# The order of the 32 small block products per pair of heads: head by head, or alternating

## The chip, the cores and the metric

The kernel runs on one core of a Trainium2 chip. The time is the device time of that core in microseconds (us), the median of several executions. Five engines work side by side, each through its own queue in order: TensorE (matmuls; PE in the profile, its weight loads PEld), VectorE (DVE), ScalarE (ACT), GpSimd (POOL) and SyncE (SP, which issues DMA transfers). They wait for each other by semaphores. Matmuls write PSUM; TensorE reads SBUF, and the other engines carry results from PSUM back to SBUF.

## The reference

A decoder trunk of two residual layers over 512 positions and 2048 channels. Layer one is gated differential attention, layer two gated RWKV-7 time mixing with 32 heads of 64 channels. What matters here is the scan of layer two, per head with state S:

```python
def step(S, inp):
    r_t, w_t, k_t, v_t, a_t, b_t = inp
    sa = jnp.einsum('bhvk,bhk->bhv', S, a_t)
    S = S * w_t[:, :, None, :] + sa[..., None] * b_t[:, :, None, :] + v_t[..., None] * k_t[:, :, None, :]
    y = jnp.einsum('bhvk,bhk->bhv', S, r_t)
    return S, y

_, ys = lax.scan(step, jnp.zeros((B, H, N, N), F32), xs)
```

Around it stand the projections `p = h @ w_in` (2048 x 8192 and some low-rank parts), a shift by one position, a normalisation per head, a gate and the projection `o @ w_out`. All of it is in float32.

## The kernel before

**Projections.** A large float32 product is made from three products of rounded parts (high by high, high by low, low by high): `mm3`, line 122. Weights come by DMA, ScalarE casts a group to its high part (`wh`, line 105) and VectorE subtracts it from the original to get the low part (`wl`, line 106). These L122 matmuls of 512 columns fill most of TensorE's time.

**The scan in chunks.** Layer two (`layer1`) takes the 32 heads as 16 pairs, head 0 of a pair on partitions 0 to 63 and head 1 on 64 to 127. The 512 positions are 8 chunks of 64. Within a chunk the recurrence is a triangular system of 64 x 64, and its inverse T is made ahead of the scan. For each pair:

- `gram` (L1304) multiplies keys by queries into the tiles `gp`, one for each head and half of the chunks; ScalarE copies them into G (L1311); sums of squares go the same way (L1210, L1211, copied at L1291). The 32 x 32 diagonal blocks go by DMA to memory (`ltd`).
- `t_solve` (L1350 to L1365) loads the diagonal blocks of all chunks and heads and inverts them on VectorE in 31 steps (L1361, L1363).
- `t_combine` puts the inverted blocks into TT by DMA, transposes the first block of each chunk on VectorE (T1, L1388), and makes the block between the two diagonal ones by two products of 32 x 32 per chunk and head. Phase one (L1394) multiplies a block of G by T1 into one half of the tile px. ScalarE copies the result to X (L1397), once per head. It also copies queries from AR over the part of G of that head that the products have read (L1400, once per head). Phase two (L1404) multiplies X by a block of TT into the other half of px, and ScalarE copies that into TT (L1407).
- `scan_pair` then goes through the chunks: L1475 (G by VS), a copy to rhs (L1478), L1486 (T by rhs), a copy to VS (L1488), L1493 (the next state), which VectorE scales and adds (L1497). `outputs` (L1515, L1519) and `centre` follow.

**Placing on the array.** The products of phase one use a 32 x 32 part of TensorE's array: rows 0 to 31 and columns 32 to 63 for head 0, rows 64 to 95 and columns 96 to 127 for head 1. Phase two uses rows 32 to 63 and columns 0 to 31 for head 0, and rows 96 to 127 and columns 64 to 95 for head 1. px is one PSUM tile of 128 x 512 (tag "pd", one buffer); the heads write different partitions of it.

**What sets the order.** A pair's chain (`chain`, `Chain.step`) is a generator that yields between its steps. Every L122 matmul of the projections that go on meanwhile counts the chain's wait down (`tick`), and when it is used up the next step's instructions are put behind that matmul (`issue_after`). GAP_D, GAP_X and GAP_T (18, 10 and 8 matmuls) are the waits in `t_combine`. All steps have a raised priority (SCAN), the casts of weights a lower raised one (AHEAD), parts of `gram` and `t_solve` a higher one (SOLVE). The queue of each engine is written at compile time by a planner: it goes through the program with its own costs for each instruction and, at each engine, takes of those that are ready the one with the highest priority, then the earliest in the program. It inserts the waits that the data need. Tiles in PSUM are tracked as wholes: the copies to X read one head's part of px, but come after both heads' products.

Two bursts per pair are meant below by "burst": the 32 instructions (each float32 product is two) of L1394 and the 32 of L1404.

Of the kernel before, what the change touches and what calls it, by code (L numbers as in the profile page):

```python
# [1137 lines left out]
NC_ = T // C  # L1138
# [233 lines left out]
def t_combine(g, j, p, lead):  # L1372

    nc, w, TT = g.nc, g.work, g.TT[j % 2]
    for h in range(2):
        for half in range(2):
            o, l0 = half * HALF, half * 16 + h * NC_
            nc.sync.dma_start(
                out=TT[h * C + o : h * C + o + HALF, :, h, o : o + HALF],
                in_=g.td[j % 2].rearrange("q (g l) t -> (q g) l t", g=NG)[:, l0 : l0 + NC_, :])  # L1380
    T1 = w.tile([P, NC_, HALF], F32, name="T1", tag="T1", bufs=1)
    X = w.tile([P, NC_, HALF], F32, name="X", tag="X", bufs=1)
    px = g.ps.tile([P, 512], F32, name="px", tag="pd", bufs=1)
    yield lead
    for h in range(2):
        r_ = slice(h * C, h * C + C)
        with g.tc.issue_after(g.centred) if g.centred else ExitStack():
            nc.vector.transpose(T1[r_], TT[r_, :, h, 0:HALF])  # L1388
    yield GAP_T
    N = NC_ * HALF  # L1390
    blocks = [(h, h * C, slice(h * C, h * C + HALF), slice(h * C + HALF, h * C + C)) for h in range(2)]
    for h, b0, lo, hi in blocks:
        for c in range(NC_):
            nc.tensor.matmul(px[hi, c * HALF : (c + 1) * HALF], p.G[lo, c, 0, h, HALF:C], T1[lo, c, :],  # L1394
                             start=True, stop=True, tile_position=(b0, b0 + HALF))
    for _, _, _, hi in blocks:
        nc.scalar.copy(X[hi], px[hi, :N].rearrange("p (c s) -> p c s", c=NC_))  # L1397
    for h, b0, _, _ in blocks:
        r_ = slice(b0, b0 + C)
        nc.scalar.copy(p.G[r_, :, 0, h, :], p.AR[r_, :, 0, :])  # L1400
    yield GAP_X
    for h, b0, lo, hi in blocks:
        for c in range(NC_):
            nc.tensor.matmul(px[lo, N + c * HALF : N + (c + 1) * HALF], X[hi, c, :], TT[hi, c, h, HALF:C],  # L1404
                             start=True, stop=True, tile_position=(b0 + HALF, b0))
    for h, b0, lo, _ in blocks:
        nc.scalar.copy(TT[lo, :, h, HALF:C], px[lo, N:].rearrange("p (c s) -> p c s", c=NC_))  # L1407
    yield GAP_T
# [46 lines left out]
def chain(g, j, p, delay, gap, gap_s, others=(), lead=GAP_D - GAP_T):  # L1455
    def steps():
        yield from t_combine(g, j, p, lead)
        yield from scan_pair(g, j, p, gap, gap_s, dict(others))

    p.chain = Chain(g, steps(), delay)  # L1460
    return p.chain
# [310 lines left out]
```

## Time and profile before

| | |
|---|---|
| median of 3 runs | 2113.84 us (2110.9 to 2114.43) |
| the profiled execution | 2111.84 us, span 2110.1 us |
| granted TensorE clock | 0.997 |
| busy: PE, DVE, ACT, POOL | 98%, 76%, 55%, 18% of the span |
| L1394, both heads | 512 instructions in 16 pairs, 18.1 us busy |
| L1404, both heads | 512 instructions in 16 pairs, 17.7 us busy |

The span is from the first to the last instruction of the profiled execution. In the groups by line, a row has the line, engine and operation, the tile written and those read, the shape, the count, then busy time in us, mean length of one in ns, and the idle time before them with what ended it. Busy time counts overlapping instructions once. A matmul's record is longer than the time until the next may start, so a group's busy time over its count is less than the mean of one. In a timeline a row has the start and length in us, the engine, the line, and how many consecutive instructions are merged; in brackets how long the engine was idle before, and what ended that.

### The profile page before, as it was taken

The numbers are of one execution on the slowest core, as the hardware profiler recorded it, in microseconds if no ns is written. First come the engines' busy times: TensorE is split into PE (matmuls) and PEld (weight loads), VectorE is DVE, ScalarE is ACT, GpSimd is POOL, SyncE is SP. The second block draws the span as 40 slices with busy tenths as digits, with TensorE's granted clock in tenths as the row PEclk, the third lists the DMA queues.
The fourth block names the chain that finished last, engine by engine and source line by source line (L and its number), as shares of the span: only waits on it lengthen the run. The fifth ranks groups of instructions, "written<-read, shape, count | busy, mean of one in ns | idle before, by whom it ended". The sixth has DMA issues, their size and how long they took to land.

```text
span 2110.1 us, 34038 instructions
## 1 busy us (share of the span) xinstructions
PE 2076.8 (98%) x11852; PEld 1690.5 (80%) x11852; DVE 1602.6 (76%) x4129; ACT 1153.6 (55%) x2278; POOL 370.4 (18%) x727
## 2 busy tenths in 40 slices
PE   9999999999999999999999999999999999999999
PEld 7888888888887788878777778888877787877887
DVE  6988888889887876576777778877777887767645
ACT  5765656566565544355465555565555556555322
POOL 1021111201112000101122221222222122221001
PEclk9999999999999999999999999999999999999999
DMA  8487877878778946623232332323333232345655
GB/s 268 153 173 190 181 170 187 166 188 177 173 183 176 307 149 179 150 88 96 90 87 89 90 90 84 94 83 92 99 95 86 85 94 86 97 138 180 190 159 121
DMA packets 159484, 294.60 MB, mean 140 GB/s; under 512 B 64352, under 2 KB 81760, under 8 KB 159312
## 3 DMA queue, kind: packets, MB, share of 16 engines
q1 hardware_dynamic: 110848, 184.91, 28.1%
q0 software_dynamic: 23808, 83.54, 21.5%
q10 hardware_dynamic: 24656, 23.97, 3.5%
q8 instruction: 93, 1.52, 0.3%
q14 instruction: 79, 0.65, 0.1%
HBM read 268.71 MB, written 23.66 MB: 139 GB/s over the span
## 4 chain that ended last, share of the span: by engine, by line
PE 74%; DVE 17%; issue 3%; ACT 3%; DMA 2%; ACTq 0%; DVEq 0%; SPq 0%
PE pp L122 33%; PE pp L568 22%; PE pt L122 4%; DVE wl L106 4%; DVE tmpl L1361 3%; DVE Tm L1363 2%; DVE VS L1497 2%; PE gp L1304 1%; ACT wh L105 1%; PE sc L122 1%; PE o L122 1%; PE sm L1475 1%; PE lora L122 1%; PE z L122 1%; PE sm L1486 1%
## 5 line engine op out<-in xcount | busy, mean ns | idle before, releaser
L106 DVE TENSOR_TENSOR wl<-wraw,wh 128x1024 fp32r<-128x1024 f32 (+2 forms) x291 | 357.7, 1229 | 211.0 <-ACT wh L105 202.2
L105 ACT CAST wh<-wraw 128x1024 fp32r<-128x1024 f32 (+2 forms) x291 | 303.6, 1043 | 266.1 <-PE pp L122 135.2
L122 PE MATMUL pp<-hL,wh 128*128 128x512 f32 x1024 | 414.7, 405 | 0.0
L122 PE MATMUL pp<-hH,wh 128*128 128x512 f32 x1024 | 413.8, 404 | 0.0
L122 PE MATMUL pp<-hH,wl 128*128 128x512 f32 x1024 | 413.6, 404 | 0.0
L122 PEld LDWEIGHTS pp<-hH,wh 128*128 128x128 f32 x1024 | 193.6, 189 | 34.3
L122 PEld LDWEIGHTS pp<-hL,wh 128*128 128x128 f32 x1024 | 193.5, 189 | 33.3
L122 PEld LDWEIGHTS pp<-hH,wl 128*128 128x128 f32 x1024 | 193.6, 189 | 32.4
L568 PE MATMUL pp<-wh,hH 128*128 128x512 f32 x448 | 176.8, 395 | 0.0
L568 PE MATMUL pp<-wh,hL 128*128 128x512 f32 x448 | 175.8, 392 | 0.0
L122 PE MATMUL pp<-wh,hH 128*128 128x512 f32 x372 | 145.6, 392 | 1.8 <-ACT hH L1092 1.8
L122 PE MATMUL pp<-wh,hL 128*128 128x512 f32 x372 | 146.4, 394 | 0.2
L122 PE MATMUL pp<-wl,hH 128*128 128x512 f32 x372 | 145.9, 392 | 0.5 <-DVE wl L106 0.5
L1481 POOL COPY SA<-VS 64x64 f32<-64x64 f32 x224 | 69.9, 312 | 425.0 <-DVE VS L1497 386.0
L1361 DVE SCALAR_TENSOR_TENSOR tmpl<-LT,Tm 128x60 f32<-128x60 f32 (+24 forms) x496 | 133.6, 269 | 11.4
L568 PE MATMUL pp<-wl,hH 128*128 128x512 f32 x448 | 140.4, 392 | 0.0
L1363 DVE TENSOR_TENSOR Tm<-Tm,tmpl 128x60 f32<-128x60 f32 (+24 forms) x496 | 104.4, 211 | 11.3
L1478 ACT COPY rhs<-sm 64x64 f32<-64x64 f32 x256 | 52.8, 206 | 89.3 <-PE sm L1475 85.9
L568 PEld LDWEIGHTS pp<-wl,hH 128*128 128x128 f32 x448 | 84.4, 188 | 17.3
L568 PEld LDWEIGHTS pp<-wh,hH 128*128 128x128 f32 x448 | 84.2, 188 | 17.3 <-issue 0.3
L568 PEld LDWEIGHTS pp<-wh,hL 128*128 128x128 f32 x448 | 84.2, 188 | 16.3
L1488 ACT COPY VS<-sm 64x64 f32<-64x64 f32 x256 | 52.7, 206 | 71.9 <-PE sm L1486 67.3
(397 smaller groups left out, 4417.6 us busy)
## 6 DMA issues: line engine op xcount, KB each, us to landing
wraw<-in_rw_w_in_dram SPq DMA_DIRECT2D x128, 512.0 KB
wraw<-in_da_w_in_dram SPq DMA_DIRECT2D x75, 512.0 KB
wraw<-in_da_w_in_dram POOLq DMA_DIRECT2D x28, 512.0 KB, 6.6
wraw<-in_da_w_out_dram SPq DMA_DIRECT2D x26, 512.0 KB
wraw<-in_rw_w_out_dram SPq DMA_DIRECT2D x26, 512.0 KB
Ta<-in_da_w_in_dram POOLq DMA_DIRECT2D x21, 512.0 KB, 5.5
Tb<-in_da_w_in_dram POOLq DMA_DIRECT2D x21, 512.0 KB, 5.5
Tc<-in_da_w_in_dram POOLq DMA_DIRECT2D x21, 512.0 KB, 5.5
```

The source lines that it names most:

```text
L105: a = nc.scalar.copy(hi[:, ks], raw[:, ks])
L106: d = nc.vector.tensor_sub(lo[:, ks], raw[:, ks], hi[:, ks].bitcast(F32))
L122: m = nc.tensor.matmul(out, a, b, start=s, stop=e, skip_group_check=skip)
L568: m = nc.tensor.matmul(out[t][:], x, wt[lo][:, k, :], start=first, stop=end and lo == 1 and k == KG - 1, skip_group_check=True)
L1304: m = nc.tensor.matmul(gp[h][:, i * P : (i + 1) * P], BK[r_, c0 + i, :, :], p.AR[r_, c0 + i, :, :], start=True, stop=True)
L1361: nc.vector.scalar_tensor_tensor(tt, LT[:, i : i + 1, i + 1 :].to_broadcast([P, s, n]), n2[:, i : i + 1], Tm[:, 0:s, i : i + 1].to_broadca ...
L1363: nc.vector.tensor_add(Tm[:, 0:s, i + 1 :], Tm[:, 0:s, i + 1 :], tt)
L1475: nc.tensor.matmul(sm[:, 0:P], both(p.G[:, c, 0]), both(VS[:, c]), start=True, stop=True)
L1478: nc.scalar.copy(rhs[r_, :], sm[r_, h * C : h * C + C])
L1481: nc.gpsimd.tensor_copy(p.SA[r_, c - 1, :], VS[r_, c, h, :])
L1488: g.copied = nc.scalar.copy(VS[r_, c, h, :], sm[r_, P : P + C])
L1497: g.state = nc.vector.scalar_tensor_tensor(VS[r_, c + 1, h, :], s_, p.gam[r_, c : c + 1], Sg[r_, :], ALU.mult, ALU.add)
```

## The change

In both phases the two loops change places: the outer one is now over the 8 chunks, the inner one over the 2 heads. Each product keeps its operands, its place on the array and its place in px. The copies around them keep their order in the program.

```diff
-    for h, b0, lo, hi in blocks:
-        for c in range(NC_):
+    for c in range(NC_):
+        for h, b0, lo, hi in blocks:
             nc.tensor.matmul(px[hi, c * HALF : (c + 1) * HALF], p.G[lo, c, 0, h, HALF:C], T1[lo, c, :],
                              start=True, stop=True, tile_position=(b0, b0 + HALF))
...
     yield GAP_X
-    for h, b0, lo, hi in blocks:
-        for c in range(NC_):
+    for c in range(NC_):
+        for h, b0, lo, hi in blocks:
             nc.tensor.matmul(px[lo, N + c * HALF : N + (c + 1) * HALF], X[hi, c, :], TT[hi, c, h, HALF:C],
                              start=True, stop=True, tile_position=(b0 + HALF, b0))
```

## The prediction

> **What bounds the kernel now.** First the head of the profile's page, for the engines' shares; then the groups of instructions by line, for the two lines that the change touches; then the stages by windows; then, around one of these places, the timelines of TensorE and ScalarE, which decide.
>
> ```profile
> span 2110.1 us, 34038 instructions
> PE 2076.8 (98%) x11852; PEld 1690.5 (80%) x11852; DVE 1602.6 (76%) x4129; ACT 1153.6 (55%) x2278; POOL 370.4 (18%) x727
> ```
>
> TensorE is busy 98% of the span, ScalarE 55%: by the averages any matmul time that is saved would be time saved. The two groups:
>
> ```profile
> L1304 PE MATMUL gp<-AR,BK 64*128 64x128 f32 x512 | 33.4, 279 | 0.7 <-DVE AR L1279 0.7
> L1394 PE MATMUL px<-T,G 32*32 32x32 f32 x512 | 18.1, 192 | 2.0 <-DVE y L1418 1.2 <-DVE T L1388 0.8
> L1404 PE MATMUL px<-TT,X 32*32 32x32 f32 x512 | 17.7, 192 | 0.0
> ```
>
> L1394 is phase one and L1404 phase two. Each product is two instructions here, so one head's eight chunks are 16 and a burst of both heads is 32; 512 make 16 bursts of each, one per pair of heads. All the small products together are 35.8 us, 1.7% of the span: that is the most there is to win from.
>
> Eleven of the 16 pairs form a steady state, with bursts from 1250.09 to 1864.22 us. The first and the last of its ten full periods, by windows (length, then PE, PEld, DVE, ACT and POOL busy, clock, DMA):
>
> ```profile
> 1250.09:1311.56 61.47, 60.67 (x422) 49.40 (x421) 46.42 (x130) 35.06 (x78) 15.24 (x35) 1.00 0.30 90
> 1802.79:1864.22 61.43, 60.75 (x422) 49.40 (x421) 45.29 (x128) 34.76 (x77) 15.27 (x35) 1.00 0.38 112
> ```
>
> Some 0.7 to 0.8 us of each period has no matmul, and busy time hides more, since a matmul's record is longer than its slot. Where TensorE waits is seen in its timeline at one of these pairs (start, length, line):
>
> ```profile
> 1557.16 1.09 PE L1394 MATMUL px<-T,G 32*32 32x32 f32 x32
> 1558.42 0.40 PE L1211 MATMUL pt<-sLx,ones 128*2 128x512 f32 x1
> 1558.74 2.06 PE L1304 MATMUL gp<-AR,BK 64*128 64x128 f32 x32
> 1560.73 1.09 PE L1404 MATMUL px<-TT,X 32*32 32x32 f32 x32
> ...
> 1564.85 0.40 PE L122 MATMUL pp<-hH,wh 128*128 128x512 f32 x1
> 1565.08 0.40 PE L122 MATMUL pp<-hL,wh 128*128 128x512 f32 x1
> 1565.41 0.43 PE L1486 MATMUL sm<-rhs,TT 128*128 128x64 f32 x2
> ```
>
> L122 matmuls start 0.23 us apart, yet the first step of the scan that needs T, L1486, starts 0.33 after its predecessor: TensorE waits about 0.10 there. ScalarE's timeline says for what:
>
> ```profile
> 1554.04 0.69 ACT L1132 ACTIVATE mixr<-pp,omu 128x512 f32<-128x512 f32 x1
> 1557.88 0.62 ACT L1400 COPY G<-AR 64x512 f32<-64x512 f32 x1 [3.15 <-PE px L1394]
> 1558.53 0.36 ACT L1397 COPY X<-px 32x256 f32<-32x256 f32 x1
> 1558.91 0.57 ACT L1291 COPY ssl<-pt 2x512 f32<-2x512 f32 x1
> 1559.51 0.36 ACT L1397 COPY X<-px 32x256 f32<-32x256 f32 x1
> 1559.90 0.61 ACT L1400 COPY G<-AR 64x512 f32<-64x512 f32 x1
> 1560.54 0.62 ACT L1101 CAST sHx<-mixr 128x512 fp32r<-128x512 f32 x1
> 1561.18 2.06 ACT L1311 COPY G<-gp 128x512 f32<-128x512 f32 x4
> 1563.09 0.74 ACT L1407 COPY TT<-px 32x256 f32<-32x256 f32 x2
> 1563.86 1.05 ACT L105 CAST wh<-wraw 128x1024 fp32r<-128x1024 f32 x1
> 1564.93 0.42 ACT L1478 COPY rhs<-sm 64x64 f32<-64x64 f32 x2
> ```
>
> From L1400 at 1557.88 to the end of L1478 at 1565.35 ScalarE has no gap: 7.47 us of work in a fixed order, and L1486 follows 0.06 behind it. So over the 8.25 us from the burst to L1486 the limit is **ScalarE's row of copies**, and not TensorE. What starts the row is head 0 alone: L1400 copies into the part of G that head 0's products of phase one read, and it comes 0.72 after the burst's start, while the burst's last matmul ends at 1.09. In the brackets stands how long ScalarE had been idle, and for whom.
>
> **The change, part by part.** Nothing is added or taken away: the same 512 matmul instructions of each line, the same copies, no DMA on any queue. Only the order within each burst changes.
>
> *How long an alternated burst takes.* No row shows it, so it is bounded. Where the two heads' halves stand apart, one head alone takes:
>
> ```profile
> 1188.11 0.69 PE L1394 MATMUL px<-T,G 32*32 32x32 f32 x16
> 1189.92 0.69 PE L1394 MATMUL px<-T,G 32*32 32x32 f32 x16
> ```
>
> Less 0.19 for the last record (L1394's mean), 15 steps take 0.50, 0.033 each. Lower end: both heads run at once, 0.69. Upper end: no overlap at all, 31 x 0.033 + 0.19 = 1.22. Today's 1.09 lies 0.13 under that: at the one change of head in the burst the second head starts while the first still runs, in the same px tile. The nearest row for steady alternation is L1304, which goes head by head within each chunk already: 32 instructions of 128 columns in 2.06 us, 0.058 each, while the same number of columns on the whole array takes 0.11 (L1475, two in 0.22 of the chain of waits, row below). That is two heads at a time. I take **0.70**: a burst is 0.39 us shorter, and 32 bursts would give 12.5.
>
> ```profile
> 1563.87 0.22 PE sm L1475 x2
> ```
>
> A rule of the Trainium skill speaks against this. The Trainium skill, TensorEngine Tiling (Array Packing), Restrictions and Gotchas, says that different row tiles cannot use one PSUM bank at the same time. The two heads here are different row tiles and both write px, whereas L1304 writes a tile per head. By that rule a burst would take 1.22 and the sum would be the second rival's below; the 0.13 of overlap in today's burst, in px too, contradicts it for a few matmuls.
>
> *What it is worth in the eleven steady pairs.* TensorE would come to L1404 0.39 earlier (X is ready then: its second copy ends at 1559.87, and L1404 would be due at 1560.34) and to L1486 0.78 earlier. There it meets ScalarE's row, whose length does not depend on this order. Its start does: head 0's last product is now the third last instruction of the burst, but if the heads run at once it still ends 0.69 to 0.70 after the start, and L1400 comes at 0.72 to 0.73. So L1486 stays at 8.25 and the wait before it grows from 0.10 to 0.88. Worth per pair: 0, bounds -0.05 (copies in another order overlap better) and +0.06 (heads hinder each other a little). I take +0.01: 11 x 0.01 = +0.1.
>
> *In the first three pairs* ScalarE has no full row; L1478 itself waits for TensorE (idle before it, in brackets):
>
> ```profile
> 1033.89 0.42 ACT L1478 COPY rhs<-sm 64x64 f32<-64x64 f32 x2 [1.51 <-PE sm L1475]
> 1085.24 0.42 ACT L1478 COPY rhs<-sm 64x64 f32<-64x64 f32 x2 [1.52 <-PE sm L1475]
> 1142.51 0.42 ACT L1478 COPY rhs<-sm 64x64 f32<-64x64 f32 x2 [1.04 <-PE sm L1475]
> ```
>
> There the saving passes on: 4 bursts x 0.39 = 1.56 in the first two. The third pair has its phase two cut by a scan step, so 0.39 for phase one and between 0 and 0.39 for the rest, say 0.20.
>
> ```profile
> 1141.34 0.71 PE L1404 MATMUL px<-TT,X 32*32 32x32 f32 x20
> 1141.98 0.49 PE L1475 MATMUL sm<-VS,G 128*128 128x128 f32 x2
> 1142.40 0.56 PE L1404 MATMUL px<-TT,X 32*32 32x32 f32 x12
> ```
>
> *In the fourth pair*, quoted above, the planner already ran head 0's 16 alone, since head 1's T1 was not there, and it will again: nothing in phase one. In phase two ScalarE's row stands in the way as in the steady state. Worth 0.
>
> *In the last pair* phase one is cut the same way. In phase two the cast that precedes L1478 waits for TensorE, so 0.39 passes on:
>
> ```profile
> 1928.08 1.05 ACT L105 CAST wh<-wraw 128x1024 fp32r<-128x1024 f32 x1 [0.67 <-PE pp L122]
> ```
>
> **Sum**, on the profiled execution of 2111.84 us (span 2110.1): -1.56 - 0.59 - 0.39 + 0.1 = -2.4, so 2109.4. The median of the runs shown is 2.0 above that execution, so the forecast for it is 2113.84 - 2.4 = **2111.4**, 0.11% less. I call anything within 0.2% (4.2 us) no change, about what a measurement of this kernel can tell.
>
> **Rivals.**
>
> *The steady pairs gain too.* The order on ScalarE is fixed at compile time by a planner that looks at what is ready. Head 0's copies become ready half a burst later in its eyes, which can move other copies. If the cast L105 (1.05 us) fell behind L1478, ScalarE's row would end early enough for TensorE's full 0.88 per pair: 11 x 0.88 = 9.7, with the 2.4 above 2101.7. If only L1101 (0.62) fell behind, 6.8 and 2104.6. For it: in the second pair L1478 has no cast ahead of it. Against it: in the fourth pair the row runs 0.6 us later against its burst (L1407 at 6.52 instead of 5.93) and the planner still put L1101 and L105 ahead of L1478:
>
> ```profile
> 1193.15 0.62 ACT L1101 CAST sHx<-mixr 128x512 fp32r<-128x512 f32 x1
> 1193.67 1.07 ACT L1311 COPY G<-gp 128x512 f32<-128x512 f32 x2
> 1194.63 0.73 ACT L1407 COPY TT<-px 32x256 f32<-32x256 f32 x2
> 1195.38 1.05 ACT L105 CAST wh<-wraw 128x1024 fp32r<-128x1024 f32 x1
> 1196.46 0.42 ACT L1478 COPY rhs<-sm 64x64 f32<-64x64 f32 x2
> ```
>
> *The heads do not overlap: slower.* If alternate matmuls run one after the other, head 0 is done after 29 x 0.033 + 0.19 = 1.15 instead of 0.69. L1400 and the whole row behind it come 0.46 later, and L1486 with them: 11 x 0.46 = 5.1. Seven bursts without that cover (six early, one in the last pair) lose 0.13 each, 0.9. Together +6.0: 2119.8. It decides as soon as a head's step grows so that its 15 steps take 0.4 us longer. For it: the two heads share px, and L1304 does not show that case. Against it: the overlap at the change of head.
>
> *The planner puts something more into the row: slower.* A ScalarE instruction of 0.6 us or more that the planner now finds ready while head 0's copies are not would push L1486 by its length: 0.69 (as L1132 before the burst) x 11 = 7.6, less 2.4: 2119.0. It outweighs the gain from 0.22 us up. For it: the planner sees half a burst more of idle time. Against it: ScalarE sat idle 3.15 us before L1400 and the planner found nothing to put there.
>
> **How the numbers follow.** Forecast (order kept, heads overlap, the steady pairs take the gain back) 0.55; steady pairs gain 0.23; no overlap 0.11; a longer row 0.11. The forecast's own range is 2109.5 to 2114.5: the early gains whole (-3.3 with -0.05 per steady pair) or only 1 us of them (with +0.06), and the runs' own spread around their median. The range for 8 in 10 takes in the faster rival and the nearer slower one: 2101.0 to 2119.0. Faster by over 0.2%: 0.22 of the first rival and 0.07 of the forecast, where the spread adds to the gain, 0.29. Slower: 0.20 of the two slower rivals. Within: 0.51.
>
> **What would show it.** Right: L1394 and L1404 bursts of 32 at 0.70 instead of 1.09; L1400 still 0.72 behind the burst; the wait before L1486 near 0.9 in the steady pairs; periods still 61.4 long. Wrong: bursts at 1.1 or more with L1400 at 1.2 (no overlap), or L1478 ahead of L105 or L1101 with periods near 60.5. The forecast fails most easily if the planner's order on ScalarE moves, since the whole steady state hangs on what stands between L1400 and L1478.

## The result, and the profile after

The kernel after takes 2108.15 us (median; 2103.75 to 2114.8) against 2113.95 (2109.42 to 2116.93) for the kernel before, run beside it 20 times each. The ratio (of the means) is 0.9976 with a 95% interval of 0.9968 to 0.9984: 0.24% faster, some 5 us, with 3.4 to 6.8 in the interval. The medians lie 5.8 apart. The profiled execution of after has a span of 2106.8 us, 3.3 less than that of before.

The head of the page of after; then, from its groups by line, those of the two changed lines (busy us, mean ns of one):

```profile
span 2106.8 us, 34037 instructions
PE 2062.7 (98%) x11852; PEld 1676.1 (80%) x11852; DVE 1602.1 (76%) x4129; ACT 1153.1 (55%) x2278; POOL 369.8 (18%) x727
```

```profile
L1394 PE MATMUL px<-T,G 32*32 32x32 f32 x512 | 11.6, 192 | 2.0 <-DVE y L1418 1.1 <-DVE T L1388 0.9
L1404 PE MATMUL px<-TT,X 32*32 32x32 f32 x512 | 11.3, 192 | 0.0
```

The bursts' busy time fell from 18.1 + 17.7 to 11.6 + 11.3 us: 12.9 us less, close to the 12.5 that the prediction gives for 32 bursts at 0.39. Yet only some 5 of them are in the time. Where the rest went is seen in the timelines of TensorE and ScalarE at the steady pair that the prediction showed (start, length, line; idle time before it in brackets):

```profile
1557.35 0.69 PE L1394 MATMUL px<-T,G 32*32 32x32 f32 x32
...
1560.52 0.69 PE L1404 MATMUL px<-TT,X 32*32 32x32 f32 x32
...
1564.48 0.40 PE L122 MATMUL pp<-hL,wh 128*128 128x512 f32 x1
1565.59 0.43 PE L1486 MATMUL sm<-rhs,TT 128*128 128x64 f32 x2 [0.71 <-ACT rhs L1478]
```

```profile
1558.08 0.62 ACT L1400 COPY G<-AR 64x512 f32<-64x512 f32 x1 [3.15 <-PE px L1394]
1558.70 0.57 ACT L1291 COPY ssl<-pt 2x512 f32<-2x512 f32 x1
1559.30 0.74 ACT L1397 COPY X<-px 32x256 f32<-32x256 f32 x2
1560.06 0.62 ACT L1400 COPY G<-AR 64x512 f32<-64x512 f32 x1
1560.70 1.07 ACT L1311 COPY G<-gp 128x512 f32<-128x512 f32 x2
1561.80 0.62 ACT L1101 CAST sHx<-mixr 128x512 fp32r<-128x512 f32 x1
1562.33 1.07 ACT L1311 COPY G<-gp 128x512 f32<-128x512 f32 x2
1563.28 0.73 ACT L1407 COPY TT<-px 32x256 f32<-32x256 f32 x2
1564.04 1.05 ACT L105 CAST wh<-wraw 128x1024 fp32r<-128x1024 f32 x1
1565.11 0.42 ACT L1478 COPY rhs<-sm 64x64 f32<-64x64 f32 x2
```

Both bursts take 0.69. L1400 still comes 0.73 behind the first, the row runs from 1558.08 to the end of L1478 at 1565.53, 7.45 us, and L1486 stands 8.24 behind the burst (8.25 before). TensorE now starts L1486 1.11 behind its predecessor instead of 0.33. In these pairs the whole gain has become a wait.

So it must have come from elsewhere. The windows of after, stage by stage, burst to burst (length; PE, PEld, DVE, ACT, POOL busy; clock; DMA): the first four pairs, the first and last steady period, the fifteenth pair, and from the last burst to the end.

```profile
1028.38:1078.98 50.60, 49.71 (x368) 38.66 (x368) 41.75 (x124) 32.39 (x76) 12.05 (x32) 1.00 0.28 82
1078.98:1138.54 59.56, 58.69 (x412) 46.63 (x411) 48.61 (x131) 33.94 (x78) 16.48 (x38) 1.00 0.32 90
1138.54:1187.42 48.88, 47.61 (x340) 37.58 (x339) 37.25 (x110) 28.52 (x69) 12.97 (x33) 1.00 0.29 86
1187.42:1250.44 63.02, 61.01 (x421) 48.85 (x420) 48.94 (x141) 35.11 (x78) 14.01 (x35) 1.00 0.31 90
1250.44:1311.82 61.38, 60.00 (x421) 48.59 (x420) 46.28 (x131) 34.96 (x78) 15.25 (x35) 1.00 0.33 92
1802.82:1864.22 61.40, 60.01 (x421) 48.58 (x421) 45.62 (x129) 34.76 (x77) 15.26 (x35) 1.00 0.38 114
1864.22:1918.79 54.57, 51.70 (x385) 40.80 (x384) 40.06 (x128) 30.60 (x72) 15.71 (x32) 1.00 0.57 172
1918.79:2106.79 188.00, 182.83 (x923) 147.93 (x923) 102.78 (x146) 64.42 (x101) 20.16 (x34) 1.00 0.58 155
```

The same stages of before, without the two steady ones that stand in the prediction:

```profile
1025.42:1078.35 52.93, 52.04 (x368) 40.60 (x368) 41.70 (x124) 32.33 (x76) 12.00 (x32) 0.97 0.26 78
1078.35:1138.73 60.38, 59.54 (x412) 47.44 (x411) 48.66 (x131) 33.97 (x78) 16.44 (x38) 1.00 0.33 89
1138.73:1188.11 49.38, 48.17 (x341) 38.37 (x340) 37.26 (x110) 28.53 (x69) 13.09 (x33) 1.00 0.27 85
1188.11:1250.09 61.98, 61.30 (x422) 49.85 (x421) 48.80 (x141) 35.07 (x78) 15.26 (x35) 1.00 0.31 92
1864.22:1921.24 57.02, 54.24 (x382) 41.05 (x381) 40.29 (x128) 30.90 (x72) 15.36 (x32) 1.00 0.56 168
1921.24:2110.08 188.84, 183.92 (x925) 149.00 (x925) 102.67 (x146) 64.31 (x101) 19.87 (x34) 1.00 0.56 154
```

| stage | after less before, us | forecast, us |
|---|---|---|
| first pair | -2.33 | -0.78 |
| second | -0.82 | -0.78 |
| third | -0.50 | -0.59 |
| fourth | +1.04 | 0 |
| ten steady periods (1250.09 to 1864.22 before, 1250.44 to 1864.22 after) | -0.35 | +0.1 |
| fifteenth | -2.45 | 0 (with the steady ones) |
| last burst to the end | -0.84 | -0.39 |
| sum | -6.25 | -2.4 |

The 3.0 us between this sum and the spans' difference lie ahead of the first burst (1025.42 and 1028.38), where the change has no instruction. In the first pair the clock column shows a second difference: 0.97 in before. For 3.4 us at the start of that stage TensorE ran at half clock, with L122 matmuls 0.43 apart instead of 0.23; nine of them start from 1026.79 to 1030.19, which makes 1.6 us. So the change itself is worth some -0.8 there, as forecast. The fourth pair and the fifteenth are what nothing in the prediction accounts for.

### The profile page after: what moved, and what is told of

The parts are those of the page before. It is cut to its first block, busy times and chain, and to the rows that moved or that the text cites. A ratio compares the mean times of both kernels' runs of the same rounds, so it can differ in the third digit from the quotient of the medians.

```text
span 2106.8 us, 34037 instructions
## 1 busy us (share of the span) xinstructions
PE 2062.7 (98%) x11852; PEld 1676.1 (80%) x11852; DVE 1602.1 (76%) x4129; ACT 1153.1 (55%) x2278; POOL 369.8 (18%) x727
## 3 DMA queue, kind: packets, MB, share of 16 engines
q8 instruction: 93, 1.52, 0.3%
## 4 chain that ended last, share of the span: by engine, by line
PE 69%; DVE 19%; ACT 5%; issue 4%; DMA 3%; ACTq 0%; DVEq 0%; SPq 0%
PE pp L122 31%; PE pp L568 21%; PE pt L122 5%; DVE wl L106 4%; DVE tmpl L1361 3%; DVE Tm L1363 3%; ACT wh L105 2%; DVE VS L1497 2%; PE gp L1304 1%; PE sc L122 1%; PE o L122 1%; DMA ys<-yTl 1%; PE sm L1475 1%; PE lora L122 1%; PE z L122 1%
## 5 line engine op out<-in xcount | busy, mean ns | idle before, releaser
L122 PE MATMUL pp<-hL,wh 128*128 128x512 f32 x1024 | 414.2, 404 | 0.0
L122 PE MATMUL pp<-hH,wl 128*128 128x512 f32 x1024 | 413.1, 403 | 0.0
L122 PE MATMUL pp<-hH,wh 128*128 128x512 f32 x1024 | 413.0, 403 | 0.0
L122 PEld LDWEIGHTS pp<-hH,wh 128*128 128x128 f32 x1024 | 193.1, 189 | 34.3
L122 PEld LDWEIGHTS pp<-hL,wh 128*128 128x128 f32 x1024 | 193.1, 189 | 33.4
L122 PEld LDWEIGHTS pp<-hH,wl 128*128 128x128 f32 x1024 | 193.2, 189 | 32.2
L122 PE MATMUL pp<-wh,hH 128*128 128x512 f32 x372 | 145.7, 393 | 2.5 <-ACT hH L1092 2.5
L122 PE MATMUL pp<-wh,hL 128*128 128x512 f32 x372 | 146.4, 393 | 0.3 <-DVE hL L1093 0.2
L122 PE MATMUL pp<-wl,hH 128*128 128x512 f32 x372 | 145.9, 392 | 0.7 <-DVE wl L106 0.5
L1478 ACT COPY rhs<-sm 64x64 f32<-64x64 f32 x256 | 52.8, 206 | 87.5 <-PE sm L1475 84.1
```

The lines of the kernel that those rows point to most:

```text
L122: m = nc.tensor.matmul(out, a, b, start=s, stop=e, skip_group_check=skip)
L1478: nc.scalar.copy(rhs[r_, :], sm[r_, h * C : h * C + C])
```

## The experiments

Theory A is the prediction's: ScalarE's row sets L1486 in the steady pairs. B is its rival: something else on TensorE or behind it sets the pace. C says that what phase one's order does to the planner makes the fourth pair's loss and the fifteenth's gain; D, that the shorter bursts themselves do, so that each phase alone would bring half. E and F concern the fifteenth pair alone: by E its own order gains, by F the time won earlier is carried there.

### The row relieved of its first and fifth copy

L1400, twice 0.62 us of the row and its start, goes to GpSimd, in the kernel before and in the kernel after:

```diff
-        nc.scalar.copy(p.G[r_, :, 0, h, :], p.AR[r_, :, 0, :])
+        nc.gpsimd.tensor_copy(p.G[r_, :, 0, h, :], p.AR[r_, :, 0, :])
```

Head by head, as before:

> Head by head as before, but the two copies L1400 of each pair (1.26 us of ScalarE's row) are made by GpSimd. Theory A (ScalarE's row from the burst to L1478 is what L1486 waits for): the row now begins with the copies to X after the whole burst, at 1.12, and is 6.2 long, so it ends near 7.4, before TensorE is due at L1486 (8.15). L1486 comes at 8.15 instead of 8.25, the period of the ten steady pairs falls from 61.41 to about 61.3, some 1 us in all. Theory B (the period is set later, by VectorE's unbroken run from the second scan step on): period unchanged at 61.4.

Alternating, as after:

> The changed kernel with the copies L1400 on GpSimd. Theory A: with the row out of the way TensorE keeps the 0.78 that the two alternated bursts save: L1486 at 7.35, the wait before it gone, the period of the steady pairs 61.37 - 0.88 = 60.5, some 9.5 us below the changed kernel over eleven pairs, near 2099. Theory B: L1486 comes earlier, but the stalls before L1475 at the fifth to seventh chunk grow by as much and the period stays at 61.4.

Head by head: 2110.97 us (10 executions), ratio to the kernel before 0.9994 (0.9981 to 1.0007), no difference. Alternating: 2097.68 (4 executions), ratio 0.9935 (0.9917 to 0.9954), which is faster than either kernel. The first and last steady period of each, by windows, head by head first:

```profile
1251.66:1312.87 61.21, 60.54 (x421) 49.47 (x420) 47.01 (x131) 33.51 (x76) 16.50 (x37) 1.00 0.33 91
1802.55:1863.77 61.22, 60.54 (x422) 49.48 (x421) 46.69 (x130) 33.34 (x75) 16.51 (x37) 1.00 0.39 114
```

```profile
1246.61:1307.02 60.41, 59.72 (x422) 48.69 (x421) 46.76 (x129) 33.64 (x76) 16.49 (x37) 1.00 0.32 91
1790.21:1850.62 60.41, 59.72 (x422) 48.68 (x421) 46.65 (x130) 33.32 (x75) 16.50 (x37) 1.00 0.40 116
```

With the row out of the way the same change of order is worth 0.80 per period, two bursts at 0.40; with the row in the way it was worth 0.03. ScalarE's and TensorE's timelines of the alternating one show the place:

```profile
1553.91 1.05 ACT L105 CAST wh<-wraw 128x1024 fp32r<-128x1024 f32 x1
1554.99 0.42 ACT L1478 COPY rhs<-sm 64x64 f32<-64x64 f32 x2
```

```profile
1548.61 0.69 PE L1394 MATMUL px<-T,G 32*32 32x32 f32 x32
...
1555.97 0.33 PE L1486 MATMUL sm<-rhs,TT 128*128 128x64 f32 x2
```

L1478 is done at 1555.41, 0.56 before L1486, which now stands 7.36 behind the burst and waits for nothing. Theory A holds for both orders; B falls. Head by head the relief is worth only 0.2 per period, 0.09 of it at L1486 (8.16 behind the burst instead of 8.25), since there TensorE had only 0.10 of wait to lose. The other 0.11 comes later in the scan and was not followed.

### One phase at a time

Phase one alternates alone, then phase two alone; the other keeps its loops as before.

```diff
     # phase one (L1394), in the first kernel; phase two (L1404), in the second
-    for h, b0, lo, hi in blocks:
-        for c in range(NC_):
+    for c in range(NC_):
+        for h, b0, lo, hi in blocks:
```

> Only phase one (L1394) alternates. Theory A: each of the first three pairs gains 0.4 (half of what both phases give), the ten steady periods stay at 61.37 to 61.41. Theory C (the 2.45 us that the fifteenth pair gains, from its burst to the next, and the 1.04 that the fourth loses come from the order that the planner writes once head 0's products of phase one end late): both are here in full, 2.4 and 1.0. Theory D (they come from the shorter bursts themselves): half of each.

> Only phase two (L1404) alternates. Theory A: 0.4 for each of the first two pairs, about 0.1 for the third, 0.4 for the last, steady periods 61.41 with the wait before L1486 grown by 0.4. Theory C: the fifteenth and the fourth pair take as long as before (57.0 and 62.0). Theory D: the fifteenth gains about 1.2, the fourth loses about 0.5.

Single times: 2107.18 and 2118.01. Fourth and fifteenth pair by windows, phase one alone first; of phase two alone also the start of the last stage:

```profile
1186.32:1249.36 63.04, 61.42 (x422) 49.26 (x421) 48.92 (x141) 35.12 (x78) 14.00 (x35) 1.00 0.31 89
1863.03:1917.52 54.49, 52.05 (x385) 41.21 (x384) 40.54 (x128) 30.59 (x72) 15.71 (x32) 1.00 0.60 174
```

```profile
1187.36:1249.33 61.97, 61.00 (x421) 49.46 (x421) 48.74 (x141) 35.06 (x78) 15.25 (x35) 1.00 0.31 92
1863.34:1922.27 58.93, 53.83 (x382) 40.66 (x381) 39.84 (x127) 30.91 (x72) 15.36 (x32) 1.00 0.54 162
1922.27:1940.00 17.73, 17.73 (x111) 13.82 (x111) 10.62 (x17) 9.60 (x20) 1.43 (x3) 0.62 0.52 158
```

Both the loss of the fourth pair and the gain of the fifteenth come with phase one; C holds and D falls. Each phase alone shortens the second pair to 59.97, half of the whole. With phase two alone the last pair's T1 came late: 3.06 us lay between the start before the last burst and that burst, 1.12 in before. Without these 1.94 the 58.93 would be 57.0, as before. After that late burst the clock stood at half for 13.7 us, so the total of that kernel cannot be compared.

In the fourth pair the trace of after shows what phase one's order did:

```profile
1187.42 0.24 PE L1394 MATMUL px<-T,G 32*32 32x32 f32 x2
...
1188.80 0.69 PE L1394 MATMUL px<-T,G 32*32 32x32 f32 x30
```

Head 1's T1 is late there. Head by head, all 16 instructions of head 0 went ahead at 1188.11; alternating, only the first product did, and head 0's other 14 instructions stand among head 1's. L1400 comes 2.05 behind the burst's start instead of 0.72, and L1486 at 8.97 instead of 8.83. That is 0.14 of the 1.04; the other 0.9 comes up again in the run with the longer row.

### The fifteenth pair

From the trace, the order of TensorE's queue in the scan of the fifteenth pair, from its fourth L1475 product on, before and after. A letter is one instruction: a is L1475, b L1486, c L1493, a dot an L122, other lines left out.

```
before  aa......bb..cc....aa..bb..cc....aa..bb..cc.....aa..bb....cc.....aa...bb
after   aa....bb....cc....aa....bb....cc....aa....bb....cc.....aa....bb...cc.....aa...bb
```

After each of these steps ScalarE or VectorE has to copy or scale before the next can start. Before, two L122 stand between many steps, and the start that follows comes 0.45 to 0.52 behind an L122 instead of 0.23: there are nine such waits in that pair's scan, and one of 0.78. After, four L122 stand between most of them, and three waits of that size are left (0.49 to 0.68). The last L1486 of the scan comes 36.62 behind the burst instead of 39.21. The next two kernels change the order in the fifteenth pair alone (j == 14), and in all others:

```diff
-    for h, b0, lo, hi in blocks:
-        for c in range(NC_):
+    for (h, b0, lo, hi), c in sorted(((x, c) for x in blocks for c in range(NC_)), key=lambda v: (v[1], v[0][0]) if j == 14 else (v[0][0], v[1])):
+        if True:
```

(j != 14 in the second; the same in both phases.)

> The products alternate in the fifteenth pair alone, in both phases; all other pairs go head by head. Its instructions on TensorE in that pair stand in the order of the kernel after (scan steps four projection matmuls apart instead of two). Theory E (that order is what gains, because the scan steps no longer come before the copies they wait for): from the fifteenth pair's burst to the last pair's burst 54.5 us instead of 57.0, every other stretch as in the kernel before (fourth pair 61.9, steady periods 61.4, first pair 51.3 without a half-clock window), total about 2.5 to 3.3 under the kernel before. Rival F (the gain is time won earlier, carried to that place): 57.0 less 0.39 or 0.78 at most, that is 56.2 to 56.6.

> The products alternate in every pair but the fifteenth. Theory E: from the fifteenth pair's burst on, the stretch takes 57.0 again; the first three pairs are short (about 50.8, 59.6, 48.9), the fourth stays at 63.0, the steady periods at 61.4. So the change is worth about 2.5 us less than whole: near 2.5 under the kernel before, half-clock windows aside. Rival F: the fifteenth stretch stays at 54.5.

Single times: 2108.93 and 2111.58. The fourth and fifteenth pair by windows, the fifteenth alone first:

```profile
1188.04:1250.03 61.99, 61.32 (x422) 49.87 (x421) 48.75 (x141) 35.09 (x78) 15.25 (x35) 1.00 0.31 91
1864.04:1918.88 54.84, 51.85 (x385) 40.81 (x384) 40.27 (x128) 30.59 (x72) 15.71 (x32) 1.00 0.58 174
```

```profile
1185.23:1248.25 63.02, 61.00 (x421) 48.85 (x420) 49.06 (x141) 35.10 (x78) 14.00 (x35) 1.00 0.31 91
1862.02:1920.15 58.13, 54.23 (x382) 41.04 (x381) 39.78 (x126) 30.91 (x72) 15.37 (x32) 1.00 0.55 163
```

With 32 instructions of each phase reordered, in one pair of sixteen, the stage takes 54.84; with all pairs but that one, 58.13. Of the 58.13, 1.32 is a later T1 of the last pair (the wait before that burst was 2.44 us, 1.12 in before); without it the stage would be 56.8, near the 57.02 of before. Its last L1486 stands at 39.01, near the 39.21 of before, and at 36.66 in the other. E holds, F falls: that pair's own order of products brings the gain. That the spacing of the scan is how it gains was not tried by itself, but all ten kernels agree: the five with the wide spacing take 53.9 to 54.8 in this stage, the five without it 56.2 to 58.9, the alternating kernel with L1400 on GpSimd among them (56.76).

The same order reaches into the last pair. From the first L1486 of that pair's scan to the last it takes 30.90 in before and 30.46 in after; it takes 30.45 where the fifteenth pair alone alternates, and 30.87 where all but that pair do. A start 0.69 behind an L122, at the scan's second L1486, is gone with it.

The gain is not the shorter bursts, which the fifteenth pair turned into a wait before L1486 like the steady ones (that start is 1.57 behind its predecessor in after, 0.79 in before).

### The row made longer

The kernel after, with head 0's copy issued twice in ten of the steady pairs:

```diff
-        nc.scalar.copy(p.G[r_, :, 0, h, :], p.AR[r_, :, 0, :])
+        for _ in range(2 if h == 0 and 3 < j < 14 else 1): nc.scalar.copy(p.G[r_, :, 0, h, :], p.AR[r_, :, 0, :])
```

> The kernel after, with head 0's copy L1400 issued twice in the ten steady pairs five to fourteen (0.62 us more in ScalarE's row, same result). Theory A (ScalarE's row sets L1486, TensorE merely waits 0.9 there): L1486 moves from 8.23 to about 8.85 behind the burst, the wait before it grows by 0.6, and each of those ten periods goes from 61.4 to 62.0: about 6 us more than the kernel after. Rival B (TensorE's wait has its own reason, and ScalarE's row has room): L1486 stays at 8.23 and the periods at 61.4.

A single time of 2120.91. Two of its ten steady periods by windows:

```profile
1247.44:1310.33 62.89, 60.43 (x421) 48.44 (x420) 46.22 (x131) 35.78 (x79) 14.09 (x35) 1.00 0.32 89
1813.55:1876.45 62.90, 60.47 (x421) 48.43 (x420) 45.80 (x130) 35.56 (x78) 14.10 (x35) 1.00 0.38 110
```

Its burst and L1486 on TensorE in the tenth pair:

```profile
1561.96 0.69 PE L1394 MATMUL px<-T,G 32*32 32x32 f32 x32
...
1570.84 0.43 PE L1486 MATMUL sm<-rhs,TT 128*128 128x64 f32 x2 [1.36 <-ACT rhs L1478]
```

L1486 stands 8.88 behind the burst instead of 8.24, and starts 1.75 behind its predecessor instead of 1.11: later by the length of the added copy, which is theory A. The periods, though, grew by 1.5 and not by 0.6. The rest is again an order: the planner put L1493 of the scan's second chunk behind two more L122 (here the order of TensorE's queue from the second L1486, a question mark for any other line):

```
kernel after, steady      bb......????..cc......aa......bb
one copy longer           bb......????....cc....aa......bb
```

L1493 then waits too (0.47 behind an L122), and two later L1475 wait longer (0.43 instead of 0.39, and 0.91 instead of 0.58). At the last L1486 the delay is 1.53. The fourth pair of after has this same order and the same three waits (0.47, 0.43, 0.91), and loses 1.04 with only 0.14 of it at L1486. So its 0.9 comes with this order, which no run changed by itself. Why the later two L1475 wait longer was not followed further.

### The two findings together

The alternating kernel with L1400 on GpSimd lacks the better spacing in the fifteenth pair (its stage took 56.76). Here L1400 stays on ScalarE in that pair:

```diff
-        nc.scalar.copy(p.G[r_, :, 0, h, :], p.AR[r_, :, 0, :])
+        (nc.scalar.copy if j == 14 else nc.gpsimd.tensor_copy)(p.G[r_, :, 0, h, :], p.AR[r_, :, 0, :])
```

> Both phases alternate and L1400 runs on GpSimd in every pair but the fifteenth, where it stays on ScalarE so that the scan steps there keep the wide spacing. Theories A and E add up: steady periods 60.4 as with all copies on GpSimd, and the fifteenth stretch near 54 instead of 56.8. Total 2.3 to 3 under the kernel with all copies on GpSimd, so about 2095, a ratio of 0.992 to the kernel before. If the spacing was not the reason, the fifteenth stretch stays at 56.8 and the ratio at 0.9935.

2094.10 us (6 executions, 2092.05 to 2097.81), ratio to the kernel before 0.9909 (0.9895 to 0.9924): the best of all. A steady period and the fifteenth pair:

```profile
1244.24:1304.66 60.42, 59.74 (x421) 48.67 (x420) 46.88 (x130) 33.62 (x76) 16.50 (x37) 1.00 0.32 91
...
1848.33:1902.27 53.94, 51.59 (x384) 40.80 (x384) 39.94 (x127) 30.60 (x72) 15.71 (x32) 1.00 0.58 173
```

Both effects are there side by side, 60.4 and 53.9. Between the two kernels with the relieved row throughout, 0.9994 head by head and 0.9935 alternating, the order is worth 0.6%, against 0.24% with the row in the way. The fifteenth pair adds 2.8 us (56.76 to 53.94), 0.13%; the ratios 0.9935 and 0.9909 lie further apart than that, but their intervals overlap.

## Why the prediction was right or wrong

The range of 2101.0 to 2119.0 holds the 2108.15, and the mechanism was right: ScalarE's row takes the gain back in the steady pairs. The size was too small: 0.11% forecast, 0.24% measured (0.16 to 0.32). By the bound of 0.2% that the prediction set itself, "no change" (chance 0.51) was missed by a hair for "faster" (chance 0.29), and the interval reaches to both sides of it. The forecast's own, narrower range of 2109.5 to 2114.5 does not hold the 2108.15. That the sum came as near as it did is in part luck, since the loss in the fourth pair offsets some of the unforeseen gain in the fifteenth.

- *How long an alternated burst takes*: forecast 0.70, measured 0.69. The heads run at once even when every matmul alternates and both write px: 32 starts within 0.50 us, one every 16 ns, against 33 ns for one head alone.
- The rule of the Trainium skill, TensorEngine Tiling (Array Packing), Restrictions and Gotchas, that different row tiles cannot use one PSUM bank at the same time, would have had the burst at 1.22; the trace differs, for two heads that write different partitions of px, and the measurement decides. The second rival (2119.8) falls with it.
- *The eleven steady pairs*: L1400 at 0.73 (forecast 0.72 to 0.73), L1486 at 8.24 (8.25), ten periods together -0.35, or -0.03 each, inside the bounds of -0.05 and +0.06. The start of L1486 behind its predecessor was forecast at a wait of 0.88, as 0.23 and the wait: 1.11. The planner did move copies, L1291 ahead of the X copies and L1101 between the L1311, but none to behind L1478, so the first rival (2101.7 or 2104.6) fell on its condition. The third rival, a longer row, did not come about either.
- *The first three pairs*: -0.8 without the clock, -0.82, -0.50, against -0.78, -0.78 and -0.59. Right.
- *The fourth pair*, "nothing in phase one", worth 0: wrong, +1.04. The step that failed is "the planner already ran head 0's 16 alone ... and it will again". In an alternated order head 0's second product stands behind head 1's first, which waits for T1, so only one product went ahead.
- *The fifteenth pair* was counted among the eleven steady ones, and that is the largest miss: 0 forecast for it, -2.45 measured. The row did take its burst gain back; but the planner's order of the scan behind it changed, from two L122 between steps to four, and with that three of ten waits were left. The prediction asked only whether copies would move on ScalarE, not whether TensorE's own order would.
- *The last pair*: -0.84 against -0.39. The first L1486 comes 0.44 earlier behind the burst; the other 0.44 lies in that pair's scan and comes with the fifteenth pair's order, as above. The output projection behind it takes as long as before.

In sum: the forecast's -2.4, another -0.4 in the early and steady terms, -1.9 in the three stages that were wrong (+1.04, -2.45, -0.45), and -1.6 for the half clock that only the profiled execution of before had in its first pair, make the -6.25 of the two traces (rounded). Without the half clock it is -4.7.

That this lies near the 5 us of the times is partly chance, since the times hold a share of the clock too. The runs list the granted clock beside each time: on the mean 0.9970 in 24 executions of the kernel before (those timed beside the experiments), 0.9977 in the 20 of the kernel after. A straight line through all of them, with one step for the change, gives 1.8 us more for each 0.001 of clock less, and leaves about 3.5 us for the change at equal clock (standard error 0.5): 0.17%, on the other side of the 0.2%. Why the traces give some 1.2 us more than that was not followed; single executions scatter by more (the first burst starts between 1023.2 and 1028.4 us in the ten traces).

## What to carry to other kernels

When a saving lies ahead of a join, price the other arm of the join first: here ScalarE's 7.45 us of copies hid 0.8 us per pair, and moving one pair of copies to GpSimd, busy 18% of the span, set them free. Where a planner writes the queues, a change of order in one place can re-space steps far behind it, with effects (-2.45 and +1.04 us in single pairs) as large as the saving itself; compare the instruction orders pair by pair before adding up durations. A short step that waits for another engine's copy wants enough independent matmuls ahead of it: two L122 were too few here, and with four most of the waits were gone.

## What the hardware showed unexpectedly

TensorE's clock fell to half for stretches of 3.4 us or a few times that. Around the first and the last burst it did so behind waits of TensorE that were shorter. In the kernel with phase two alone alternating, around the last burst, by windows:

```profile
1918.00:1922.10 4.10, 1.08 (x5) 0.41 (x4) 1.24 (x3) 1.14 (x2) 0.00 (x0) 1.00 0.78 205
1922.10:1935.80 13.70, 13.53 (x90) 10.39 (x91) 8.05 (x13) 5.97 (x12) 0.00 (x0) 0.50 0.50 156
```

There 3.06 us lay between the last start ahead of the burst and the burst (waits are measured so in this section). It happened at the last burst in three other kernels as well, behind waits of 1.22, 2.44 and 2.53 us, and not in six, behind 1.04 to 1.52. At the first burst it happened in three of the four kernels with that pair's phase one head by head (waits of 1.46 to 1.59), and in none of the six with it alternating (1.45 to 1.78).

The stretches of one execution start on a fixed grid: by the clock record of the trace they begin at 685.41 and 1026.75 in before, 100 times 3.413 us apart, and at 686.48, 1027.81 and 1922.10 with phase two alone alternating, 100 and 262 times apart. It is the same in the other traces with several stretches. The Trainium skill, TensorE: Matmul & The Clock Gate, Part 1: The HAM clock gate, gives a free-running window of about 3.4 us and says that the clock is halved after an idle window; the length of the stretches and their grid agree, but the idle time at these two bursts was below a window each time. Whether alternating makes the fall rarer stays open: each kernel shows it in one execution. The clocks listed with the times lean that way, 0.9970 on the mean of 34 executions head by head and 0.9977 of 30 alternating (L1400 on either engine), with single executions scattering by 0.001. A stretch at the first burst costs some 1.6 us.
